# The first pass of a decoder trunk's first SwiGLU layer, written anew: modulation sums on TensorE, another order of each step

## The chip, the cores and the metric

The kernel runs on one core of a Trainium2 chip. The metric is the device time of one execution in microseconds (us), the median of several executions. The engines of the core are TensorE (PE in the profile; PEld is its weight loading), VectorE (DVE), ScalarE (ACT), GpSimd (POOL) and SyncE (SP), which issues most of the transfers.

## The reference

Two layers act on 512 tokens of width 1024 in fp32. Each has a SwiGLU half-step, a mixing step and another SwiGLU half-step, and each of these begins with an RMS norm and a modulation whose shift and scale come from a conditioning vector `c`. Only the head of the first half-step matters here:

```
h    = rms_norm(x, g)                        # x: (1, 512, 1024)
ada  = silu(c) @ ada_w + ada_b               # 9 x 1024 numbers a layer: shift, scale, gate of three steps
h    = h * (1.0 + scale) + shift             # per column of the 1024
out  = (silu(h @ w_gate) * (h @ w_up)) @ w_down     # w_gate, w_up: 1024 x 2816
```

`silu(c) @ ada_w` is a product of a vector with a matrix: each of its numbers is a sum over 1024 rows of `ada_w`, which come from memory 1 MB at a time.

## The kernel before

**Layout.** `x` is kept transposed, as eight tiles x0 to x7 of 128 columns (on the partitions) by 512 tokens. A product with a weight matrix is made in blocks: 128 rows of the weight by 128 output columns are the stationary operand, 512 tokens stream past it. fp32 accuracy comes from three products in a reduced format (fp32r): `mac` issues hi·hi (L302), hi·lo (L303: weight hi, data lo) and lo·hi (L304: weight lo, data hi) for each block. A weight's hi part is a cast on ACT (L284), its lo part a subtraction on DVE, or on POOL for an item with `pool_low` (both L286). An *item* is the weight for 128 output columns with all eight row blocks; `gu[0]`, `gu[1]`, ... are those of gate and up in turn (even ones gate, odd ones up).

**Order.** The whole program is one list of calls, `self.plan`; every engine takes its instructions in the order in which the list issues them, and semaphores join the engines. Raw weights arrive in four buffers of 1 MB (`RAW_BUFS`), loaded on SP's queue in the order of use; a buffer is loaded again once all uses of what it held have been issued. `hold` keeps a lo part back until `release`; `late` splits an item only where the list says `pre`.

**The first pass.** The modulation of this first half-step can't be had before `ada_w` lands, so the pass goes column block by column block. For block `d` (128 of the 1024 columns), `first_blocks` makes shift and scale from one raw buffer [128, 8, 2, 128] (row block k, shift or scale j):

- `scaled(d)`: three terms on ACT (L1516), raw times one number of `silu(c)` per partition;
- `products(d)`: the other five on DVE (L1524) into two of the three sums, and two additions that join the three (L1527, L1528; on DVE for d up to 1, on POOL after that);
- `sums(d)`: the sum over the partitions, two one-column products on PE with a vector of ones (L1535), and three small DVE operations that make `modB` (the shift, L1539) and `modA` ((1 + scale)·g, L1540, L1541).

Then `apply` modulates that column block: `t = x·modA·rb` on DVE (L575; `rb` is the reciprocal norm of each token), `hh = t + modB` rounded on ACT (L578), and `hl`, what the rounding left, on DVE (L580, kept back until `low`). Its 512-token products follow: 12 for the four *lead* items (`gu[0]` to `gu[3]`), and from column 1 on (`JOIN`) also 9 for the three *join* items (`gu[4]` to `gu[6]`), which have caught up on column 0 by then. Over all eight columns that is 168 products. The next item, `gu[7]`, follows with all its columns at hand. In every step the list issues `sums(k + 1)` and `apply(k + 1)` **ahead of** the products of column k, so that column k's 21 products run on PE while DVE and ACT make column k + 1. Everything behind the first pass is the same code before and after.

## Time and profile before

| | us |
|---|---|
| time, median of 3 runs (1841.98 to 1844.58) | 1843.25 |
| profiled execution, own time | 1845.38 |
| profiled execution, span of the trace | 1843.6 |
| TensorE busy in the span | 1794.6 |
| first pass: first 512-token product starts | 23.08 |
| `gu[7]`'s first product starts | 83.12 |

The span is the time from the first to the last instruction in the trace; the execution's own time has 1.8 us around it. Durations below are those of one instruction in the trace; since PE's instructions overlap their neighbours, what a product costs in a run is the distance from one start to the next. A window's "PEclk" is TensorE's granted clock as a share of full speed: 1.00 is 2.4 GHz, 0.50 is 1.2 GHz.

### The profile page before, as it was taken

The page shows a single profiled execution, that of the slowest core. Times are in us where ns is not written, and L with a number is a line of the kernel's source. Part 1 is how long each engine was busy: PE and PEld are TensorE (multiplying, and loading weights), DVE is VectorE, ACT ScalarE, POOL GpSimd, SP SyncE. Part 2 cuts the span into 40 slices and gives each one's busy share as a digit, 9 for nine tenths or more (in the row PEclk, how much of TensorE's full clock was granted, in tenths as well). Part 3 has the DMA queues.
Part 4 walks back from the last instruction along what each step waited for, and adds up shares of the span by engine and source line. Part 5 has one row for each costly group of instructions (what it writes and reads, how often), then busy time and mean ns, then how long its engine had stood idle before and what let it go on. Part 6 is the DMA issues. An engine that isn't in the chain of part 4 may idle for free.

```text
span 1843.6 us, 26711 instructions
## 1 busy us (share of the span) xinstructions
PE 1794.6 (97%) x10730; PEld 1563.4 (85%) x10730; DVE 1411.1 (77%) x2084; ACT 816.1 (44%) x1404; POOL 144.5 (8%) x123
## 2 busy tenths in 40 slices
PE   5999999999999999999999999999999999999998
PEld 3787889988778888989888889998866788898997
DVE  6689879775797869799677787886898586485874
ACT  4322325447754433436344234453545444253543
POOL 2100000005760000000000000000002000000000
PEclk7999999999999999999999999999999999999999
DMA  9585564447752346353423664543462132424321
GB/s 253 164 295 205 172 187 122 138 115 164 166 177 88 115 162 196 123 148 105 160 71 113 218 210 136 145 133 97 134 205 71 54 92 69 114 81 126 92 92 46
DMA packets 275940, 255.93 MB, mean 139 GB/s; under 512 B 5628, under 2 KB 254312, under 8 KB 275816
## 3 DMA queue, kind: packets, MB, share of 16 engines
q1 hardware_dynamic: 273380, 245.78, 43.5%
q0 software_dynamic: 2304, 8.39, 2.5%
q8 instruction: 84, 1.38, 0.3%
q14 instruction: 40, 0.33, 0.1%
q10 hardware_dynamic: 132, 0.05, 0.0%
HBM read 243.72 MB, written 2.10 MB: 133 GB/s over the span
## 4 chain that ended last, share of the span: by engine, by line
PE 81%; DVE 10%; ACT 3%; issue 2%; POOL 2%; DMA 1%; SPq 0%; ACTq 0%; POOLq 0%; DVEq 0%
PE bank L791 30%; PE bank L302 16%; PE bank L304 16%; PE bank L303 16%; DVE hl L580 1%; DVE wlo L286 1%; DVE adaacc L487 1%; DMA raw<-in_ada_w_dram 1%; ACT whi L284 1%; DVE t L575 1%; POOL y L1124 1%; DVE pm L1362 1%; DVE x L1010 1%; DVE p L1359 0%; DVE acc L1524 0%
## 5 line engine op out<-in xcount | busy, mean ns | idle before, releaser
L302 PE MATMUL bank<-th,whi 128*128 128x512 f32 (+1 forms) x896 | 336.6, 376 | 0.7 <-ACT th L1404 0.7
L304 PE MATMUL bank<-th,wlo 128*128 128x512 f32 (+1 forms) x896 | 333.9, 373 | 2.7 <-POOL wlo L286 2.7
L303 PE MATMUL bank<-tl,whi 128*128 128x512 f32 (+1 forms) x896 | 333.4, 372 | 1.1 <-DVE tl L687 0.9
L302 PE MATMUL bank<-hh,whi 128*128 128x512 f32 (+1 forms) x864 | 322.1, 373 | 5.5 <-ACT hh L578 3.2
L303 PE MATMUL bank<-hl,whi 128*128 128x512 f32 (+1 forms) x864 | 316.6, 366 | 8.1 <-DVE hl L580 8.1
L304 PE MATMUL bank<-hh,wlo 128*128 128x512 f32 (+1 forms) x864 | 315.8, 366 | 3.2 <-DVE wlo L286 2.6
L284 ACT CAST whi<-raw 128x1024 fp32r<-128x1024 f32 (+1 forms) x205 | 204.4, 1012 | 135.8 <-PE bank L303 83.3
L286 DVE TENSOR_TENSOR wlo<-raw,whi 128x1024 fp32r<-128x1024 f32 (+1 forms) x179 | 209.4, 1187 | 19.1 <-ACT whi L284 18.4
L304 PEld LDWEIGHTS bank<-th,wlo 128*128 128x128 f32 x896 | 169.4, 189 | 36.1 <-POOL wlo L286 4.3
L303 PEld LDWEIGHTS bank<-tl,whi 128*128 128x128 f32 x896 | 169.6, 189 | 32.3 <-DVE tl L687 1.3
L302 PEld LDWEIGHTS bank<-th,whi 128*128 128x128 f32 x896 | 169.6, 189 | 32.0 <-ACT th L1404 0.9
L303 PEld LDWEIGHTS bank<-hl,whi 128*128 128x128 f32 x864 | 163.4, 189 | 37.9 <-DVE hl L580 9.6
L302 PEld LDWEIGHTS bank<-hh,whi 128*128 128x128 f32 x864 | 163.6, 189 | 36.9 <-ACT hh L578 3.3
L304 PEld LDWEIGHTS bank<-hh,wlo 128*128 128x128 f32 x864 | 163.7, 189 | 33.2 <-DVE wlo L286 3.7
L1010 DVE SCALAR_TENSOR_TENSOR x<-bank,modG,x 128x512 f32<-128x512 f32 (+1 forms) x124 | 85.7, 698 | 133.2 <-PE bank L304 132.3
L791 PE MATMUL bank<-f,qhi 128*128 128x256 f32 x896 | 165.3, 282 | 0.0
L791 PE MATMUL bank<-f,whi 128*128 128x256 f32 x896 | 163.0, 280 | 0.2
L748 ACT CAST qhi<-raw 128x512 fp32r<-128x512 f32 x168 | 100.7, 621 | 111.9 <-issue 77.1
L487 DVE SCALAR_TENSOR_TENSOR adaacc<-raw,cond,adaacc 128x1024 f32<-128x1024 f32 x112 | 143.7, 1283 | 2.7
L791 PEld LDWEIGHTS bank<-f,whi 128*128 128x128 f32 x896 | 137.6, 188 | 1.9 <-ACT yy L851 0.9
L791 PEld LDWEIGHTS bank<-f,qhi 128*128 128x128 f32 x896 | 138.7, 190 | 0.0
L791 PE MATMUL bank<-f,qlo 128*128 128x256 f32 x448 | 126.5, 282 | 0.2 <-DVE qlo L751 0.2
(247 smaller groups left out, 3334.8 us busy)
## 6 DMA issues: line engine op xcount, KB each, us to landing
raw<-in_ada_w_dram SPq DMA_DIRECT2D x64, 1024.0 KB, 5.0
raw<-in_ffn_w_down_dram SPq DMA_DIRECT2D x32, 1024.0 KB, 5.5
raw<-in_ffn_w_gate_dram SPq DMA_DIRECT2D x58, 512.0 KB, 4.1
raw<-in_ffn_w_up_dram SPq DMA_DIRECT2D x58, 512.0 KB, 5.3
raw<-in_ffn_w_gate_dram SPq DMA_DIRECT2D x15, 1024.0 KB, 5.4
raw<-in_ffn_w_up_dram SPq DMA_DIRECT2D x15, 1024.0 KB, 5.4
raw<-in_ffn_w_down_dram SPq DMA_DIRECT2D x16, 768.0 KB, 4.4
raw<-in_conv_w_in_dram SPq DMA_DIRECT2D x20, 512.0 KB, 5.9
```

Source lines behind the costliest of these rows:

```text
L284: self.nc.scalar.copy(hi[:, 0:n, :], w)
L286: low = lambda eng=eng, lo=lo, hi=hi, w=w, n=n: eng.tensor_tensor(lo[:, 0:n, :], w, hi[:, 0:n, :].bitcast(F32), op=ALU.subtract)
L302: nc.tensor.matmul(ps, lhsT=it.hi[k], rhs=xh[:, sl], start=start, stop=False)
L303: nc.tensor.matmul(ps, lhsT=it.hi[k], rhs=xl[:, sl], start=False, stop=False)
L304: nc.tensor.matmul(ps, lhsT=it.lo[k], rhs=xh[:, sl], start=False, stop=stop)
L487: nc.vector.scalar_tensor_tensor(acc, r.tile[:, j, :], self.cond[:, k:k + 1], acc, op0=ALU.mult, op1=ALU.add)
L575: nc.vector.scalar_tensor_tensor(t, self.x[k][:, sl], self.modA[:, i, k:k + 1], rb, op0=ALU.mult, op1=ALU.mult)
L580: self.pend = lambda: nc.vector.scalar_tensor_tensor(self.hl[k][:, sl], t, b, self.hh[k][:, sl].bitcast(F32), op0=ALU.add, op1=ALU.subtract)
L748: self.nc.scalar.copy(hi, src)
L791: mm = lambda w, x, start=False: nc.tensor.matmul(ps, lhsT=w, rhs=x, start=start, stop=False, skip_group_check=True)
L1010: nc.vector.scalar_tensor_tensor(self.x[d][:, sl], ps[:, sl], self.modG[:, i, d:d + 1], self.x[d][:, sl], op0=ALU.mult, op1=ALU.add)
L1124: nc.gpsimd.tensor_tensor(y, y, m, op=ALU.add)
```

## The change

Only the first pass is changed.

- **Sums.** `by_pe(d)` says how many of the eight terms stay on ACT and DVE: 2, 2, 3, 5, 6, 6, 6, 6 for d = 0 to 7, the first on ACT, the others on DVE into the same sum. PE makes the rest: one-column fp32 products with the raw block as the stationary operand and a column of `silu(c)` as the moving one, and one with ones for the sum of ACT and DVE (L1559), for the scale (j = 1) first and then the shift. Per column that is 14, 14, 12, 8, 6, 6, 6, 6 one-column products, 72 in all, where there were 2 each, 16 in all. The additions on DVE and POOL are gone. `modA` is now one DVE operation (L1561; `one_b`, 1 + bias, is made once), `modB` one on ACT (L1563).
- **Order.** `sums(k + 1)` and `apply(k + 1)` stand **behind** the lead products of column k, and the join products between `apply(k + 1)` and the lead products of column k + 1. The join items start later and apart (`JOINS`: at k = 2, 4 and 7) and run one column behind. With column 1 only `gu[0]` and `gu[2]` go on; `gu[1]` and `gu[3]` take columns 0 and 1 together.
- **Buffers.** The three join items' raw weights go into buffers that are idle then (`fetch_home`), not into the ring of four.
- **Products that nothing reads.** `busy(n)` issues n products of the identity with itself (L1527): 8 while x arrives, 4 ahead of the norm's spread, 6 behind `sums(0)` and 6 behind `sums(1)`.

```diff
+    def fetch_home(self, items):
+
+        for it in items:
+            r, n = it.raw, len(it.raw.home)
+            r.tile = []
+            for e, tag in enumerate(r.home):
+                if tag == "s13":
+                    t = self.fp.tile([P, 2, S], F32, name=tag, tag=tag, bufs=1).rearrange("p a b -> p (a b)")
+                elif tag == "adaacc":
+                    t = self.fp.tile([P, D], F32, name=tag, tag=tag, bufs=1)
+                else:
+                    t = self.fp.tile([P, S], F32, name=tag, tag=tag, bufs=3)
+                t = t.rearrange("p (a b) -> p a b", b=P)
+                self.nc.sync.dma_start(t, r.src[:, e * ND // n:(e + 1) * ND // n, :])
+                r.tile += [t[:, a:a + 4, :] for a in range(0, ND // n, 4)]
...
+            w = src[i] if isinstance(src, list) else src[:, i * step:(i + 1) * step, :]
...
+        self.busy(BUSY[0])
...
+            nc.vector.tensor_scalar(self.one_b, self.adabT[:, 0, 8:16], 1.0, None, op0=ALU.add)
...
+    def busy(self, n):
+
+        ps = self.bank()
+        for _ in range(n):
+            self.nc.tensor.matmul(ps[:, 0:P], lhsT=self.ident, rhs=self.ident, start=True, stop=True)
+        self.free(ps)
...
         def scaled(d):
             def go():
-                st[d] = acc = [self.fp.tile([P, S], F32, name=f"acc{e}", tag=SPARE[d % 3 * 3 + e], bufs=1)
-                               [:, 0:256].rearrange("p (a b) -> p a b", a=2) for e in range(3)]
-                for k in range(3):
-                    nc.scalar.activation(acc[k], raws[d].tile[:, k], AF.Copy, scale=self.cond[:, k:k + 1])
+                st[d] = acc = self.fp.tile([P, S], F32, name="acc0", tag=SPARE[d % 3], bufs=1)[
+                    :, 0:256].rearrange("p (a b) -> p a b", a=2)
+                nc.scalar.activation(acc, raws[d].tile[:, 0], AF.Copy, scale=self.cond[:, 0:1])
             return go
 
         def products(d):
             def go():
                 acc = st[d]
-                for k in range(3, 8):
-                    a = acc[k % 2]
-                    nc.vector.scalar_tensor_tensor(a, raws[d].tile[:, k], self.cond[:, k:k + 1], a,
+                for k in range(1, by_pe(d)):
+                    nc.vector.scalar_tensor_tensor(acc, raws[d].tile[:, k], self.cond[:, k:k + 1], acc,
                                                    op0=ALU.mult, op1=ALU.add)
-                eng = nc.gpsimd if d > DMERGE else nc.vector
-                eng.tensor_tensor(acc[2], acc[2], acc[0], op=ALU.add)
-                eng.tensor_tensor(acc[2], acc[2], acc[1], op=ALU.add)
             return go
 
         def sums(d):
             def go():
                 ps = self.bank()
-                for j in range(2):
-                    nc.tensor.matmul(ps[:, j:j + 1], lhsT=st[d][2][:, j, :], rhs=self.ones[:, 0:1],
-                                     start=True, stop=True)
-                b = self.adabT[:, 0, d:d + 1], self.adabT[:, 0, 8 + d:9 + d]
-                m = self.modA[:, 0, d:d + 1]
-                nc.vector.tensor_tensor(self.modB[:, 0, d:d + 1], ps[:, 0:1], b[0], op=ALU.add)
-                nc.vector.scalar_tensor_tensor(m, ps[:, 1:2], 1.0, b[1], op0=ALU.add, op1=ALU.add)
-                nc.vector.tensor_tensor(m, m, self.g_of(0, 0)[:, d:d + 1], op=ALU.mult)
+                for j in (1, 0):
+                    terms = [(raws[d].tile[:, k, j, :], self.cond[:, k:k + 1]) for k in range(by_pe(d), 8)]
+                    terms.append((st[d][:, j, :], self.ones[:, 0:1]))
+                    for n, (w, c) in enumerate(terms):
+                        nc.tensor.matmul(ps[:, j:j + 1], lhsT=w, rhs=c, start=n == 0,
+                                         stop=n == len(terms) - 1)
+                nc.vector.scalar_tensor_tensor(self.modA[:, 0, d:d + 1], ps[:, 1:2], self.one_b[:, d:d + 1],
+                                               self.g_of(0, 0)[:, d:d + 1], op0=ALU.add, op1=ALU.mult)
+                nc.scalar.activation(self.modB[:, 0, d:d + 1], ps[:, 0:1], AF.Identity,
+                                     bias=self.adabT[:, 0, d:d + 1], scale=1.0)
...
-        for it, q in zip(join, (4, 6, 2)):
+        for it, home in zip(join, (("s13",), ("adaacc",), ("qlo", "qlo"))):
+            it.raw.home = home
+        for it, q in zip(join, (4, 2, 6)):
             it.store = [(self.th[q + e], self.tl[q + e]) for e in range(2)]
             it.late = True
         for it in [(lead + join)[e] for e in LOWS]:
@@ -1566,38 +1591,55 @@
         def ready(k):
             return lambda: self.apply(0, k, FULL, self.rb0)
         self.call(lambda: self.start_copy(range(7)))
-        self.call(scaled(0))
-        self.call(products(0), raws[0])
+        self.call(lambda: self.busy(BUSY[1]))
         self.call(self.start_spread)
+        self.call(scaled(0), raws[0])
+        self.call(products(0))
         self.call(self.early)
         self.call(lambda: self.start_copy((7,)))
         for e in HOLD:
             lead[e].hold = True
+        lead[1].late = lead[3].late = True
+        self.call(sums(0), raws[0])
+        self.call(lambda: self.busy(BUSY[2]))
+        self.call(lambda: self.fetch_home(join[:1]))
+        self.pre([lead[0]])
+        self.call(ready(0))
+        self.call(self.low)
         self.pre([lead[0], lead[2]])
-        self.call(sums(0))
-        self.call(ready(0))
         self.call(self.release)
-        self.call(self.low)
         self.call(scaled(1), raws[1])
-        self.call(products(1), raws[1])
+        self.call(products(1))
         self.outer([lead[0], lead[2]], 0, None, True, False)
-        self.pre(lead)
-        if EARLY:
-            self.call(self.release)
+        fetches = [lambda e=e: self.fetch_home(join[e:e + 1]) for e in (1, 2)]
         for k in range(ND):
+            if k > 1:
+                self.outer(lead, k, None, False, k == 7)
+            if k < 2:
+                self.call(fetches[k])
+            if k + 1 < ND:
+                self.call(sums(k + 1), raws[k + 1])
+                if k == 0:
+                    self.call(lambda: self.busy(BUSY[3]))
+                self.call(ready(k + 1))
+                self.call(self.low)
+            if k == 0:
+                self.outer([lead[0], lead[2]], 1, None, False, False)
+                self.pre(lead)
+                self.call(self.release)
+            for it, first in zip(join, JOINS):
+                if k == first - 1:
+                    self.pre([it])
             if k + 2 < ND:
                 self.call(scaled(k + 2), raws[k + 2])
-            if k + 1 < ND:
-                self.call(sums(k + 1))
-                self.call(ready(k + 1))
-            self.call(self.release)
-            if k + 2 < ND:
-                self.call(products(k + 2), raws[k + 2])
-            self.call(self.low)
-            self.outer(lead if k else [lead[1], lead[3]], k, None, k == 0, k == 7)
-            if k >= JOIN:
-                for q in range(0 if k == JOIN else k, k + 1):
-                    self.outer(join, q, None, q == 0, q == 7)
+                self.call(products(k + 2))
+            if k == 0:
+                for q in range(2):
+                    self.outer([lead[1], lead[3]], q, None, q == 0, False)
+            for it, first in zip(join, JOINS):
+                if k >= first:
+                    for q in range(0 if k == first else k - 1, k if k < 7 else 8):
+                        self.outer([it], q, None, q == 0, q == 7)
...
-JOIN = 1
+JOINS = (2, 4, 7)
+BUSY = (8, 4, 6, 6)
+def by_pe(d):
+    return (2, 2, 3, 5)[d] if d < 4 else 6
```

Three places show the new order. On TensorE, around the first column's sums (`bank_279`/`bank_272`: sums of column 0; `hh_101`, `hl_109`: column 0; `acc`: the sum that ACT and DVE made), before:

```order
L1498 MATMUL bank_256<-ident,rs_162 128x128 x4
L419 MATMUL bank_263<-ident,par 128x32
L420 MATMUL bank_263<-ident,adab 128x72
L1535 MATMUL bank_279<-ones,acc_242 128x1 x2
L302 MATMUL bank_312<-hh_101,whi 128x512
L303 MATMUL bank_312<-hl_109,whi 128x512
L304 MATMUL bank_312<-hh_101,wlo 128x512
L302 MATMUL bank_316<-hh_101,whi 128x512
L303 MATMUL bank_316<-hl_109,whi 128x512
L304 MATMUL bank_316<-hh_101,wlo 128x512
L1535 MATMUL bank_328<-ones,acc_292 128x1 x2
```

The same place now (column 1's sums write `bank_329`):

```order
L1517 MATMUL bank_255<-ident,rs_172 128x128 x4
L436 MATMUL bank_265<-ident,par 128x32
L437 MATMUL bank_265<-ident,adab 128x72
L1559 MATMUL bank_272<-cond,raw 128x1 x6
L1559 MATMUL bank_272<-ones,acc_262 128x1
L1559 MATMUL bank_272<-cond,raw 128x1 x6
L1559 MATMUL bank_272<-ones,acc_262 128x1
L1527 MATMUL bank_292<-ident 128x128 x6
L318 MATMUL bank_319<-hh_101,whi 128x512
L319 MATMUL bank_319<-hl_109,whi 128x512
L320 MATMUL bank_319<-hh_101,wlo 128x512
L318 MATMUL bank_323<-hh_101,whi 128x512
```

The two sums of a column have become fourteen products with raw weights and ones, and the unread products with `ident` stand behind them. In the middle of the pass, TensorE at the sums of column 6 before (`bank_580`); `hh_105` is column 4, `hh_106` column 5:

```order
L303 MATMUL bank_414<-hl_113,th_120 128x512
L304 MATMUL bank_414<-hh_105,tl_128 128x512
L1535 MATMUL bank_580<-ones,acc_530 128x1 x2
L302 MATMUL bank_312<-hh_106,whi 128x512
L303 MATMUL bank_312<-hl_114,whi 128x512
L304 MATMUL bank_312<-hh_106,wlo 128x512
L302 MATMUL bank_348<-hh_106,whi 128x512
L303 MATMUL bank_348<-hl_114,whi 128x512
L304 MATMUL bank_348<-hh_106,wlo 128x512
L302 MATMUL bank_316<-hh_106,whi 128x512
```

and now (`bank_578`; `bank_319`, and others of its kind, belong to the lead items, `bank_468` and `bank_553` to the join items):

```order
L320 MATMUL bank_385<-hh_106,wlo 128x512
L1559 MATMUL bank_578<-cond,raw 128x1 x2
L1559 MATMUL bank_578<-ones,acc_543 128x1
L1559 MATMUL bank_578<-cond,raw 128x1 x2
L1559 MATMUL bank_578<-ones,acc_543 128x1
L318 MATMUL bank_468<-hh_105,th_122 128x512
L319 MATMUL bank_468<-hl_113,th_122 128x512
L320 MATMUL bank_468<-hh_105,tl_130 128x512
L318 MATMUL bank_553<-hh_105,th_120 128x512
L319 MATMUL bank_553<-hl_113,th_120 128x512
L320 MATMUL bank_553<-hh_105,tl_128 128x512
L318 MATMUL bank_319<-hh_107,whi 128x512
```

Before, the products of column 5 followed the sums of column 6 at once; now only the joins' six stand between the sums of column 6 and lead products that need column 6. On VectorE in the same part of the program, before (`t_448` and `hl_112`: column 3):

```order
L1539 TENSOR_TENSOR modB<-bank_442,adabT 128x1
L1540 SCALAR_TENSOR_TENSOR modA<-bank_442,adabT 128x1
L1541 TENSOR_TENSOR modA<-modA,vec 128x1
L575 SCALAR_TENSOR_TENSOR t_448<-x_96,modA,sq 128x512
L1524 SCALAR_TENSOR_TENSOR acc_437<-raw,cond,acc_437 128x256
L1524 SCALAR_TENSOR_TENSOR acc_436<-raw,cond,acc_436 128x256
L1524 SCALAR_TENSOR_TENSOR acc_437<-raw,cond,acc_437 128x256
L1524 SCALAR_TENSOR_TENSOR acc_436<-raw,cond,acc_436 128x256
L1524 SCALAR_TENSOR_TENSOR acc_437<-raw,cond,acc_437 128x256
L580 SCALAR_TENSOR_TENSOR hl_112<-t_448,modB,hh_104 128x512
L1539 TENSOR_TENSOR modB<-bank_488,adabT 128x1
```

and now:

```order
L594 SCALAR_TENSOR_TENSOR t_457<-x_96,modA,sq 128x512
L599 SCALAR_TENSOR_TENSOR hl_112<-t_457,modB,hh_104 128x512
L1548 SCALAR_TENSOR_TENSOR acc_461<-raw,cond,acc_461 128x256 x5
L1561 SCALAR_TENSOR_TENSOR modA<-bank_487,one_b,vec 128x1
L594 SCALAR_TENSOR_TENSOR t_498<-x_97,modA,sq 128x512
L599 SCALAR_TENSOR_TENSOR hl_113<-t_498,modB,hh_105 128x512
```

The five additions for a later column stood between `t` and `hl` of a column; now `hl` follows `t`, and the additions follow `hl`.

## Rows read from the trace of the kernel before

**Rows 1.** The profile's page: busy time of TensorE, its granted clock in 40 slices of the span (tenths), and the chain that ended last by engine.

```profile
PE 1794.6 (97%) x10730; PEld 1563.4 (85%) x10730; DVE 1411.1 (77%) x2084; ACT 816.1 (44%) x1404; POOL 144.5 (8%) x123
...
PEclk7999999999999999999999999999999999999999
...
PE 81%; DVE 10%; ACT 3%; issue 2%; POOL 2%; DMA 1%; SPq 0%; ACTq 0%; POOLq 0%; DVEq 0%
```

**Rows 2.** Windows of the first pass by stage. Columns: window, its length, then busy time (and instructions) of PE, PEld, DVE, ACT, POOL, then granted clock, DMA share, GB/s.

```profile
14.90:18.00 3.10, 0.00 (x0) 0.00 (x0) 2.12 (x6) 2.33 (x6) 0.00 (x0) 0.93 1.16 316
18.00:23.00 5.00, 0.99 (x4) 0.93 (x4) 3.90 (x9) 2.62 (x4) 2.35 (x1) 0.50 1.14 323
23.00:26.50 3.50, 3.17 (x6) 1.78 (x6) 3.47 (x9) 3.17 (x6) 0.00 (x0) 0.50 1.18 292
26.50:34.70 8.20, 4.24 (x11) 2.51 (x10) 6.38 (x12) 3.42 (x8) 4.30 (x3) 0.50 1.00 250
34.70:41.40 6.70, 6.65 (x18) 5.39 (x19) 5.53 (x12) 3.84 (x7) 2.59 (x3) 0.50 0.42 116
41.40:44.80 3.40, 1.14 (x6) 0.61 (x4) 3.40 (x3) 0.02 (x1) 2.73 (x2) 0.99 1.00 264
44.80:48.30 3.50, 3.50 (x9) 2.73 (x10) 0.48 (x1) 1.30 (x3) 0.00 (x0) 0.51 1.16 308
48.30:82.00 33.70, 33.50 (x152) 26.30 (x150) 20.86 (x48) 9.49 (x18) 7.67 (x8) 1.00 0.58 168
```

**Rows 3.** TensorE's waits from 12 to 90 us: line, engine and tile waited for; total, times, longest.

```profile
PE bank L1535 <- DVE acc L1528: 4.4, 2, 4.1
PE bank L302 <- ACT hh L578: 3.2, 1, 3.2
PE bank L304 <- DVE wlo L286: 2.6, 2, 2.0
PE bank L304 <- DVE tl L286: 2.3, 1, 2.3
PE bank L1535 <- POOL acc L1528: 1.6, 1, 1.6
```

**Rows 4.** Timeline of the start: start, duration, engine, line, operation, count, and idle time before with what ended it.

```profile
14.93 1.31 ACT L1516 ACTIVATE acc<-raw,cond 128x256 f32<-128x256 f32 x3 [0.86 <-DMA raw<-in_ada_w_dram]
15.88 2.07 DVE L1524 SCALAR_TENSOR_TENSOR acc<-raw,cond,acc 128x256 f32<-128x256 f32 x5 [1.55 <-ACT acc L1516]
...
18.89 0.99 PE L1535 MATMUL bank<-ones,acc 128*128 128x1 f32 x4 [4.08 <-DVE acc L1528]
19.05 2.35 POOL L286 TENSOR_TENSOR wlo<-raw,whi 128x1024 fp32r<-128x1024 f32 x1 [5.34 <-ACT whi L284]
...
22.31 0.72 ACT L578 ACTIVATE hh<-t,modB 128x512 fp32r<-128x512 f32 x1 [2.38 <-DVE t L575]
...
23.08 0.80 PE L302 MATMUL bank<-hh,whi 128*128 128x512 f32 x1 [3.21 <-ACT hh L578]
23.32 0.75 DVE L580 SCALAR_TENSOR_TENSOR hl<-t,modB,hh 128x512 fp32r<-128x512 f32 x1
...
24.57 2.00 ACT L284 CAST whi<-raw 128x1024 fp32r<-128x1024 f32 x2 [0.33 <-DMA raw<-in_ffn_w_up_dram]
...
25.14 0.63 PE L302 MATMUL bank<-hh,whi 128*128 128x512 f32 x1
...
25.57 0.63 PE L303 MATMUL bank<-hl,whi 128*128 128x512 f32 x1
...
26.96 0.93 PEld L1535 LDWEIGHTS bank<-ones,acc 128*128 128x128 f32 x4 [1.06 <-issue]
...
27.77 0.33 PEld L302 LDWEIGHTS bank<-hh,whi 128*128 128x128 f32 x1
```

**Rows 5.** Timeline of one step at full clock, around the sums of a column in the middle of the pass.

```profile
54.93 0.52 PEld L1535 LDWEIGHTS bank<-ones,acc 128*128 128x128 f32 x4 [0.47 <-POOL acc L1528]
...
55.37 0.19 PEld L302 LDWEIGHTS bank<-hh,whi 128*128 128x128 f32 x1
...
55.57 0.16 DVE L1539 TENSOR_TENSOR modB<-bank,adabT 128x1 f32<-128x1 f32 x1 [1.30 <-PE bank L1535]
...
55.72 0.40 PE L303 MATMUL bank<-hl,whi 128*128 128x512 f32 x1
...
55.83 0.16 DVE L1541 TENSOR_TENSOR modA<-modA,vec 128x1 f32<-128x1 f32 x1
55.95 0.39 PE L304 MATMUL bank<-hh,wlo 128*128 128x512 f32 x1
...
56.03 0.75 DVE L575 SCALAR_TENSOR_TENSOR t<-x,modA,sq 128x512 f32<-128x512 f32 x1
...
56.81 0.73 ACT L578 ACTIVATE hh<-t,modB 128x512 fp32r<-128x512 f32 x1 [3.70 <-DVE t L575]
```

**Rows 6.** TensorE's timeline at another place of the kernel, where eight narrow fp32 weight loads and products run in a row.

```profile
488.06 0.95 PE L1183 MATMUL bank<-blk,sq 128*128 128x2 f32 x8
488.88 0.48 PE L302 MATMUL bank<-hh,whi 128*128 128x512 f32 x1
```

**Rows 7.** TensorE's timeline at the first and the third product of `gu[7]`.

```profile
83.12 0.50 PE L302 MATMUL bank<-hh,whi 128*128 128x512 f32 x1 [0.87 <-ACT whi L284]
...
84.38 0.50 PE L304 MATMUL bank<-hh,wlo 128*128 128x512 f32 x1 [0.53 <-DVE wlo L286]
```

More of the change, by code (lines that the diff above doesn't have):

```diff
@@ L39, in __init__ @@
         self.shape, self.src, self.uses = shape, src, uses
-        self.tile = None
+        self.tile = self.home = None
 class Item:
@@ L144, in touch @@
                 def touch(r):
-                    if id(r) not in known:
+                    if r.home is None and id(r) not in known:
                         known.add(id(r))
@@ L154, in used @@
                     touch(r)
-                else:
+                elif r.home is None:
                     uses[id(r)] -= 1
@@ L281, in split @@
         for i, (hi, lo) in enumerate(parts):
-            w = src[:, i * step:(i + 1) * step, :]
+            w = src[i] if isinstance(src, list) else src[:, i * step:(i + 1) * step, :]
             n = w.shape[1]
@@ L442, in setup @@
         self.early, self.fetch, self.rest = early, fetch, rest
+        self.one_b = cp.tile([P, ND], F32, name="one_b")
         self.modA = cp.tile([P, 6, ND], F32, name="modA")
@@ L1507, in first_blocks @@
         w = self.a["ada_w"][0].rearrange("(k p) (t e) -> p k t e", p=P, t=9)
-        raws = [Raw([P, 8, 2, P], w[:, :, 0:2, d * P:(d + 1) * P], 2 - (d == 0)) for d in range(ND)]
+        raws = [Raw([P, 8, 2, P], w[:, :, 0:2, d * P:(d + 1) * P], 2) for d in range(ND)]
         st = {}
@@ L1730 @@
 HOLD = (1, 2)
-DMERGE = 1
 EARLY = 0
```

## The prediction

> **What bounds the kernel now.** I read the page first: TensorE is busy for 97% of the span and makes 81% of the chain that ended last [rows 1]. So the reader looks for time in which PE does no 512-token product, or does it slowly. The granted clock is below full only in the first of the 40 slices [rows 1]; everything that is changed ends at `gu[7]`, about 84 us in, and behind that the code and the order are the same. I therefore compare one point, the start of `gu[7]`, before and after; what it moves by, the end moves by, since PE is the bound from there on.
>
> The windows [rows 2] split the first pass. At full clock a 512-token product takes 0.23 us from start to start (55.72 to 55.95, [rows 5]), at half clock 0.43 (25.14 to 25.57, [rows 4]). Before 48.3 us the clock is mostly at 0.50: PE runs 6 products and then parts of two windows with 11 and 18 instructions at half, and 9 more at 0.51 after a dip. Less the eight sums instructions that the middle two hold, some 36 products lose 0.20 each, about 7 us, and the first sums about 0.4 a pair: 8 us go to the clock. From 48.3 to 82 PE is busy 33.5 of 33.7 us at full clock: there is nothing to gain there.
>
> The waits [rows 3]: 4.1 us for the first column's `acc` on DVE, 3.2 for the first `hh`, 2.0 and 2.3 for lo parts on DVE, 1.6 for `acc` on POOL, and the rest short ones. The pass so consists of 168 products, 16 one-column products, the half clock and waits. `gu[7]`'s first product starts at 83.12 after a wait, and its third at 84.38 after another [rows 7]; as if all ran on from the third, it starts at 84.38 - 0.46 = 83.92.
>
> **The change, part by part.**
>
> *One-column products.* 72 instead of 16. A pair costs 0.44 (55.37 - 54.93, four weight loads, [rows 5]); in a run of eight loads 0.82 (488.06 to 488.88, [rows 6]), that is 0.205 for a product of two loads; at half clock 0.405 (26.96 to 27.77, [rows 4]). 72 x 0.205 = 14.8 us against 3.5: **11.3 us more of PE's time**, all on the path, as nothing else can stand in its place on PE. What it costs with a raw block as stationary operand no row shows. From above it is 0.22 (the pair alone, halved: 15.8 us in all); from below, if one of its two loads hid beside the other, 0.10 (7.4 us in all). I take 0.205, since the loads of [rows 6] have the same shape and type. The additions on DVE and POOL that go are off the path once the first `acc` is there (DVE's additions cost 0.41 each, [rows 4], and stand behind `hl` now).
>
> *The chain behind the sums.* Before, column k's 21 products cover it. After, `modA` waits for the last one-column product, S. From [rows 5]: the first small DVE operation starts 0.17 to 0.20 after the last sum, `t` 0.2 later (one operation instead of three), `hh` 0.78 after that (56.03 to 56.81) and takes 0.73, PE starts about 0.05 later: S + 1.93. `hl` takes 0.75 (23.32, [rows 4]) from S + 1.91, so the second product, which reads it, starts at S + 2.72. Twelve lead products then end at S + 5.27 when nothing covers them. Join products between them only fill the 1.9 us, they don't add.
>
> *The start.* The first fourteen one-column products begin when the raw block lands (14.93, [rows 4]), no longer at 18.89: S0 = 14.93 + 2.87 = 17.80. `hh` waits for a cast on ACT as well, so the first product starts near 20.3 instead of 23.08. POOL's lo part (2.35 us, [rows 4]) behind that cast holds the third; the six products of column 0 end at 23.1. Column 1: S1 = 23.1 + 2.87 = 26.0, second product 28.7, six end 29.9. `gu[1]` and `gu[3]` land at 24.57 [rows 4]; their casts (1.0 each) now stand behind column 1's `hh`, which ends at 27.5, so POOL's lo part of `gu[3]` ends about 32 (27.5 + 2.0 + 2.35); with the seven of their twelve products that are left then, 33.9.
>
> *The steps at full clock.* S2 = 33.9 + 12 x 0.205 = 36.4. Column 2 has nothing to cover it: S3 = 36.4 + 5.27 + 8 x 0.205 = 43.3. S4 = S3 + 5.27 + 6 x 0.205 = 49.8. S5 = S4 + 5.27 + 1.23 + 0.4 for an `acc` that five additions make late = 56.7. At k = 4 fifteen join products (3.5 us) hide the chain: S6 = 56.7 + 27 x 0.232 + 1.23 = 64.2. S7 = 64.2 + 6.5 = 70.7. The last lead products end at 75.9, 36 join products take 8.35, and `gu[7]` starts at **84.3**; its parts are ready by then, so the waits of [rows 7] are gone. Against 83.92 that is **+0.4**: 11.3 us of sums, 2.5 at most of unread products behind the two first sums (12, each no dearer than a 512-token one) that lie in the chain's wait, and about 13 us of chain waits, against 8 of clock and 16 of old waits.
>
> *The clock.* That is for a clock that holds. The rows: at the start it is high, then goes to 0.50 while PE does nothing until the first sums (window 14.9 to 18 at 0.93 with no PE work, 18 to 23 at 0.50 with 0.99 us busy). It doesn't rise in 26.5 to 34.7, with PE busy for 4.24 of 8.2 us, part of it one-column products. It is back at 0.99 in 41.4 to 44.8, behind a window in which PE was busy 6.65 of 6.7. And there, with PE busy for 1.14 of 3.4 us around a single wait of 2.3 [rows 3], it is lost again: 0.51 in the next [rows 2]. After the change the first 17 us have nothing to hurt more; but from 23.1 to 28.6 PE has one 512-token product at most, else fourteen one-column and six unread ones, and from 33.9 to 39 twelve one-column ones and one wide. Whether narrow products count as work no row shows alone. Bounds: they count in full, no loss (+0.4); they count for nothing, loss in both places and at the start. The nearest row is the dip at 44 us, so I take a loss in both later places: fourteen sums at 0.405 instead of 0.205, the products of column 1 and a part of the next twelve at 0.43 instead of 0.23, of which the wait for POOL absorbs some: sums 2 start near 36.7 (**+2.8**); around column 2 some eight products at half clock: **+1.6**. Sum: 0.4 + 2.8 + 1.6 = **+4.8**. If the first fall stays at 17.5 too, column 0's six products and the unread ones add 1.9.
>
> The Trainium skill, page "TensorE: Matmul & The Clock Gate", section "Why this matters for your kernels", advises to keep the engine busy and to leave no long idle gap between bursts of products, and names an idle gap as what takes the clock. With the unread products the gaps here are short, so by that page the clock would hold and the result be the +0.4. The trace differs from it in one place: one wait of 2.3 us between products sufficed [rows 2, 3].
>
> **Transfers.** About 10.5 MB stand behind the first block on SP's queue; at 0.25 to 0.32 MB per us [rows 2] the last block lands near 50 to 55 us, well ahead of column 7's sums at 64. Hidden.
>
> **The rivals.**
> A. *The clock holds* (the unread products do what narrow work can): +0.4 us. For it: a window with PE busy got the clock back. Against: the dip at 44.
> C. *The clock falls at the first sums too*, as before: +6.7. For it: the first window of [rows 2].
> F. *The chain starts at the scale's column, not at the last product.* The scale is summed first; if `t` starts when it is there, the shift's seven to three one-column products run beside DVE's `modA` and `t`: (7 + 7 + 6 + 4 + 3 + 3 + 3) x 0.205 = 6.8 us off the +0.4 at full clock, about **-6.2**; faster from some 4.1 us saved. Against it: `modA` is written after the whole group in the list, and in [rows 5] the DVE operation that reads the second sum stands with the first behind the pair. A shorter price for the one-column products would act the same way: it takes 0.06 us a product.
> D. *No change*: each gain is taken back. It is A's number.
>
> **How the numbers follow.** The sum is against the profiled execution's own 1845.4 us (span 1843.6): 1850.2. That is 2.1 above the median of the runs, 1843.25; the shift of +4.8 carried to the median gives **1848.0**. 0.2% is 3.7 us, about what a measurement of this kernel tells from no change. Chances: the forecast B 0.48, A 0.22, C 0.12, F 0.14, rest 0.04. B is uncertain by 2 either way (a quarter of it falls within 3.7); A by 2.5. Faster: F, 0.02 of A and 0.02 of the rest, 0.18. Same: 0.20 of A, 0.12 of B, 0.02 of the rest: 0.34. Slower: 0.36 of B and C: 0.48. The range goes from 1841.0 (A's lower edge, which leaves out F) to 1851.5 (C with 1.5 more); for B alone it is 1846 to 1850.
>
> **What would show it.** In the profile after: first 512-token product at 20 to 21 us; granted clock near 0.5 from 24 to 34 and again around 39 to 44; PE idle before `hh` in each step by 1 to 2.5 us except where the fifteen join products stand; steps of 6.5 to 7.5 us against 5.6 before (33.7 us for six columns, [rows 2]); no wait at `gu[7]`; its start near 88.7 us. It is wrong if one-column products take far from 0.2, if the clock is at 1.0 throughout (then the start is 84 to 85), or if `t` starts before the shift's products have ended.

## Result and the profile after

The changed kernel is slower: 1861.89 us (median of 4 runs, 1860.59 to 1866.14) against 1842.83, a ratio of 1.0106 (95% interval 1.0091 to 1.0121). The forecast was 1848.0, with a range up to 1851.5. The profiled execution has a span of 1858.8 us, 15.2 more than that of before, while the medians differ by 19.1: the profiled execution of before took 2.55 us more than this median of before, and the one here 1.30 less than its own. The page, its lines that answer to [rows 1]:

```profile
span 1858.8 us, 26972 instructions
...
PE 1818.2 (98%) x10890; PEld 1588.2 (85%) x10890; DVE 1401.9 (75%) x2053; ACT 811.3 (44%) x1396; POOL 132.1 (7%) x111
...
PEclk8999999999999999999999999999999999999999
...
PE 81%; DVE 10%; ACT 4%; issue 2%; POOL 2%; DMA 1%; SPq 0%; POOLq 0%; ACTq 0%; DVEq 0%
```

TensorE is as full as before and its clock even better; the loss must lie in more work, or in dearer work. Windows of the first pass, cut where the granted clock changes (columns as in [rows 2]), and TensorE's waits (as [rows 3]):

```profile
14.10:18.00 3.90, 3.90 (x35) 3.88 (x35) 1.28 (x6) 1.56 (x5) 0.00 (x0) 1.00 1.11 346
18.00:23.60 5.60, 3.02 (x15) 2.14 (x15) 4.44 (x4) 2.99 (x5) 2.36 (x1) 0.90 1.11 362
23.60:32.40 8.80, 8.80 (x43) 8.71 (x41) 1.53 (x3) 1.58 (x3) 0.00 (x0) 0.50 1.03 302
32.40:38.00 5.60, 4.69 (x20) 3.58 (x20) 4.28 (x4) 1.70 (x3) 2.46 (x1) 0.97 0.48 140
38.00:43.00 5.00, 3.09 (x26) 2.83 (x24) 1.32 (x3) 1.36 (x3) 0.00 (x0) 1.00 1.10 324
43.00:46.40 3.40, 3.15 (x8) 2.37 (x8) 3.29 (x7) 1.06 (x3) 0.00 (x0) 0.50 0.89 265
46.40:91.40 45.00, 40.97 (x201) 32.57 (x201) 25.95 (x47) 14.89 (x27) 2.60 (x2) 1.00 0.40 125
```

```profile
PE bank L318 <- ACT hh L597: 5.0, 6, 1.9
PE bank L319 <- DVE hl L599: 3.3, 6, 1.9
PE bank L320 <- POOL wlo L302: 0.9, 1, 0.9
PE bank L1559 <- DVE acc L1548: 0.5, 1, 0.5
```

The clock is at half from 22.5 to 32.8 and from 43.0 to 46.4, 14 us in place of 27 [rows 2]. The waits have changed as forecast: the long one for the first `acc` is gone, one for `hh` and one for `hl` stand in nearly every step. The places that answer to [rows 4, 5 and 7], first the start (four rows of the timeline), then one step, then `gu[7]`:

```profile
19.10 2.36 POOL L302 TENSOR_TENSOR wlo<-raw,whi 128x1024 fp32r<-128x1024 f32 x1 [5.82 <-ACT whi L300]
...
19.68 2.33 DVE L599 SCALAR_TENSOR_TENSOR hl<-t,modB,hh 128x512 fp32r<-128x512 f32 x1 [1.10 <-ACT hh L597]
...
19.70 0.49 PE L318 MATMUL bank<-hh,whi 128*128 128x512 f32 x1 [0.71 <-ACT hh L597]
...
22.06 0.50 PE L319 MATMUL bank<-hl,whi 128*128 128x512 f32 x1 [1.87 <-DVE hl L599]
```

```profile
54.68 0.51 PE L1559 MATMUL bank<-cond,raw 128*128 128x1 f32 x4
...
55.72 0.36 PE L1559 MATMUL bank<-ones,acc 128*128 128x1 f32 x2
...
57.99 0.51 PE L318 MATMUL bank<-hh,whi 128*128 128x512 f32 x1 [1.11 <-ACT hh L597]
58.78 0.51 PE L319 MATMUL bank<-hl,whi 128*128 128x512 f32 x1 [0.28 <-DVE hl L599]
```

```profile
91.41 0.39 PE L318 MATMUL bank<-hh,whi 128*128 128x512 f32 x1
```

The sums start at 14.1, the first 512-token product at 19.70 (23.08 before), but the second waits until 22.06 for `hl`, which takes 2.33 us on DVE while POOL makes a lo part. In the step, the sums end at 55.94, three join products follow, then waits of 1.11 and 0.28. `gu[7]` starts without a wait at 91.41: **8.3 us later than in [rows 7]**, 7.4 to 7.5 when the two waits there are counted in.

So half of the 15.2 us lies behind the first pass, where no order and no instruction was changed. The place of [rows 6] shows it on the way (the same sums, 406 us behind `gu[7]`):

```profile
497.50 0.95 PE L1202 MATMUL bank<-blk,sq 128*128 128x2 f32 x8
```

488.06 has become 497.50, a lag of 9.4 us; from `gu[7]` to the end the lag grows evenly (this growth is called the drift below), but for two places where the clock of before is at half. Behind `gu[7]` a 512-column product takes 234.2 ns from start to start. The first and the 61st of a run without a gap in this kernel, 14.05 us for 60:

```profile
102.42 0.40 PE L320 MATMUL bank<-hh,wlo 128*128 128x512 f32 x1
...
116.47 0.40 PE L320 MATMUL bank<-hh,wlo 128*128 128x512 f32 x1
```

### The profile page after: what moved, and what is told of

Same layout as the page of the kernel before. It is cut to its first block, busy times and chain, and to the rows that moved or that the text cites. A ratio compares the mean times of both kernels' runs of the same rounds, so it can differ in the third digit from the quotient of the medians.

```text
span 1858.8 us, 26972 instructions
## 1 busy us (share of the span) xinstructions
PE 1818.2 (98%) x10890; PEld 1588.2 (85%) x10890; DVE 1401.9 (75%) x2053; ACT 811.3 (44%) x1396; POOL 132.1 (7%) x111
## 4 chain that ended last, share of the span: by engine, by line
PE 81%; DVE 10%; ACT 4%; issue 2%; POOL 2%; DMA 1%; SPq 0%; POOLq 0%; ACTq 0%; DVEq 0%
PE bank L810 30%; PE bank L319 16%; PE bank L318 16%; PE bank L320 16%; DVE hl L599 2%; DVE adaacc L506 1%; DVE wlo L302 1%; PE bank L1559 1%; ACT whi L300 1%; DVE t L594 1%; DVE pm L1381 1%; POOL y L1143 1%; DVE p L1378 1%; POOL wlo L302 1%; ACT hh L597 1%
## 5 line engine op out<-in xcount | busy, mean ns | idle before, releaser
L302 DVE TENSOR_TENSOR wlo<-raw,whi 128x1024 fp32r<-128x1024 f32 (+1 forms) x179 | 208.9, 1183 | 20.1 <-ACT whi L300 19.1
L319 PEld LDWEIGHTS bank<-hl,whi 128*128 128x128 f32 x864 | 163.4, 189 | 42.2 <-DVE hl L599 13.7
```

Of the source, the lines that this page charges most:

```text
L302: low = lambda eng=eng, lo=lo, hi=hi, w=w, n=n: eng.tensor_tensor(lo[:, 0:n, :], w, hi[:, 0:n, :].bitcast(F32), op=ALU.subtract)
L319: nc.tensor.matmul(ps, lhsT=it.hi[k], rhs=xl[:, sl], start=False, stop=False)
```

## Experiments

The kernel before was measured again beside each group of experiments: 1842.8 to 1843.5 us. Ratios are to that.

**Addresses.** A program places its tiles one behind the other. The new tile `one_b` (32 bytes in each partition) stands ahead of the raw and weight tiles and moves them up by 32 bytes: `whi` from 122336 to 122368, while `hh`, `hl`, `th` and `tl` stay (`hh` at 19616). Theory 1: this makes every product dearer. Rival 2: the new first pass does.

e1 puts an unused tile of the same size into the kernel before:

```diff
+        self.pad = cp.tile([P, ND], F32, name="pad")
         self.modA = cp.tile([P, 6, ND], F32, name="modA")
```

> The kernel before with one unused tile of 32 bytes per partition allocated where the changed kernel has one_b (ahead of modA), so that the raw, hi and lo weight tiles lie 32 bytes higher, at the very addresses of the changed kernel; no instruction differs. Behind the first pass the changed kernel's trace falls back by another 7.8 us, evenly over the rest of the program (a product's start-to-start 233.3 ns before, 234.2 after). Theory 1 (addresses): this kernel shows that drift alone: 7 to 10 us above the kernel before, start-to-start 234.2 ns, first product and gu[7] as before (23.1, 83.1). Rival 2 (the drift comes with the new first pass, its instruction count or the moments at which the clock changes): within 2 us of the kernel before, 233.3 ns.

Measured: 1854.99 us, ratio 1.0063 (1.0051 to 1.0075): +12.1. Not one instruction is added, `gu[7]` stands where it stood, and the sums of [rows 6] are 2.0 us late (490.10); at the end the lag is 8.4 (span 1852.0). The other 3.7 lie in which executions were profiled: that of before 2.5 above its median, that of e1 1.2 below. The first row is `gu[7]`, the second from another window:

```profile
83.18 0.50 PE L302 MATMUL bank<-hh,whi 128*128 128x512 f32 x1 [0.87 <-ACT whi L284]
...
490.10 0.95 PE L1184 MATMUL bank<-blk,sq 128*128 128x2 f32 x8
```

e2 takes the shift out of the changed kernel:

```diff
-        self.one_b = cp.tile([P, ND], F32, name="one_b")
+        self.one_b = self.vec[:, 96:96 + ND]
```

> The changed kernel with one_b in eight unread columns of the tile vec, so that all weight tiles lie where they lay before; order and products as in the changed kernel. Theory 1: 1852 to 1855 us, start-to-start back at 233.3 ns, gu[7] at about 91 us as in the changed kernel, and no drift behind it. Rival 2: 1861 us, 234.2 ns.

Measured: 1854.27 us, 1.0057 (1.0044 to 1.007), 7.6 below the changed kernel and 11.4 above before. `gu[7]` starts at 92.38, no earlier, and the drift is gone: `gu[7]` is 8.5 behind before (with the waits there counted in), and the end 8.3, by the spans. Sixty products take 14.00 us, 233.3 ns each:

```profile
102.42 0.39 PE L319 MATMUL bank<-hl,whi 128*128 128x512 f32 x1
...
116.42 0.39 PE L319 MATMUL bank<-hl,whi 128*128 128x512 f32 x1
```

Theory 1 stands. The new first pass as a whole (sums, order, buffers and unread products) costs 8.3 us by itself in the traces, 11.4 in the medians. e3, e7, e8 and e16 ask what of the address counts; they move tiles by other amounts (one_b as [P, 16]; the unused tile as [P, 48]; one of [P, ND] ahead of x; cond and mx moved ahead of x).

> The changed kernel with one_b twice as large, so that the weight tiles lie 64 bytes higher than before instead of 32. Theory 1 with a period of 64 bytes: 1852 to 1855 us, 233.3 ns. Theory 1 with a longer period or none: the drift stays in another size. Rival 2: 1861 us, 234.2 ns.

> The kernel before with an unused tile of 192 bytes ahead of modA: raw and weight tiles move by 192 bytes, and then lie at the same address modulo 512 as the tiles hh, hl, th and tl. Products with weights in th ran in the changed kernel at 227 ns from start to start, those with weights in whi at 233 (no shift), 234 (32 bytes) and 232.5 (64 bytes). If the relative address of weight and data modulo 512 sets the rate: 227 ns all through, 30 to 45 us faster than before. If 32 bytes modulo 64 is all that counts: as before within 2 us. Otherwise some other rate, total between 1842 and 1862.

> The kernel before with an unused tile of 32 bytes ahead of x, so that data (x, hh, hl, th, tl) and weights all move by 32 bytes and keep their distance. If the distance of weight and data sets the rate: as before within 2 us (233.3 ns). If the weight's own address does: +10 to +13 us as in e1 (234.2 ns). If the data's address does: another rate.

> The kernel before with the two 32-byte tiles cond and mx allocated ahead of x instead of behind the data tiles: data tiles 64 bytes higher, weights where they were, so weight less data is 256 modulo 512 (0 modulo 256), where it was 320 before and is 0 in e7. If the distance counts modulo 256: the 512-column products run at 228 ns and the time is 6 to 12 us below the kernel before, as in e7. If modulo 512: another rate, and no such gain.

| run | whi less hh, modulo 256 | 512-column product, ns | 256-column, ns | total, us (ratio to before) |
|---|---|---|---|---|
| before, e2 | 64 | 233.3 | 117.0 | 1843, 1854.27 |
| e8, all moved by 32 | 64 | 233.3 | 117.0 | 1843.41 (0.9999, 0.999 to 1.0008) |
| changed, e1 | 96 | 234.2 | 118.0 | 1861.89, 1854.99 |
| e3 | 128 | 232.5 | 118.6 | 1861.59 (1.0099, 1.0086 to 1.0112) |
| e7 | 0 | 227.8 | 118.4 | 1834.28 (0.9955, 0.9941 to 0.9968) |
| e16 | 0 (256 modulo 512) | 227.7 | 118.4 | 1835.06 (0.9954, 0.994 to 0.9967) |

The nanoseconds are mean distances from one start to the next in stretches behind 100 us; a single run without a gap can lie up to 0.8 lower (e7's sixty below: 227.0). e8 says that for the 512-column products the distance of the two operands counts and not their place; e16, that a distance of 256 modulo 512 does as well as one of 0, since e7 and e16 agree. My three expectations for e7 all missed in size: the 512-column products became 5.5 ns cheaper, as the first said, but the 256-column ones 1.4 dearer, and 9 us were left. The 256-column figure is a mean over unlike kinds: in these traces (mean steps of 100 to 130 ns) those of `hh`, `hl`, `th` or `tl` with `whi` or `wlo` took 114.1 to 115.1 ns at a distance of 64, 117.4 to 118.5 at 96, 118.5 to 119.6 at 128 and 119.3 to 119.9 at 0, while those of `f` moved by 1.4 at most. For the former 64 was the cheapest of the four. The table's rates, times the 4296 products with 512 columns and 6048 with 256 that the trace holds, give an estimate of +9.9 us for e1, +6.2 for e3 against e2 and -15 for e7; measured were +12.1, +7.3 and -9.0, so the signs come out, the size of e7 doesn't. Sixty products of e7, 13.62 us:

```profile
117.52 0.39 PE L303 MATMUL bank<-hl,whi 128*128 128x512 f32 x1
...
131.14 0.39 PE L303 MATMUL bank<-hl,whi 128*128 128x512 f32 x1
```

e12 also put the tiles of the phase pool (f, qhi) at the same place modulo 512 (the tile tab moved to the pool ahead, 160 bytes of pad).

> The kernel before with 192 bytes (an unused tile of 160 and the one-number tile tab, moved from another pool) ahead of modA: raw and weight tiles at 160 modulo 512 as in e7, and the tiles of the phase pool (f, qhi and others) at 160 modulo 512 too, where they lay at 192 in e7 and at 0 before. 256-column products took 117.0 ns from start to start before, 118.4 in e7; those of the commonest short kind 113. If the relative address of the two operands sets the rate there as well: 113 to 115 ns and 10 to 20 us below e7 (1834.3). If not: 1834 within 2 us.

It missed: 1840.5 us (0.9983, 0.9974 to 0.9992), above e7, with 256-column products at 119.8 ns. For the 256-column products, equal places are not the cheapest; why, stays open. e13 gives the changed kernel e7's distance (one_b as [P, 48]).

> The changed kernel with one_b 192 bytes large instead of 32, so that raw and weight tiles lie at 160 modulo 512, like the data tiles, as in e7; nothing else differs from the changed kernel. If the distance of weight and data is all that the drift is: e2's time less what e7 gained, 1854.3 - 9.0 = 1845 (1843 to 1848), a 512-column product at 228 ns, and gu[7] at 91 to 92.5 us as in e2. Rival (the changed kernel drifts for another reason as well): above 1850.

1842.76 us (0.9996, 0.9987 to 1.0005), 0.2 below its range, the 512-column product at 227.8, `gu[7]` at 91.98: 160 bytes of unused space take 19.1 us off the changed kernel. The sum of the parts closes only roughly: e1's 12.1 and e2's 11.4 make 23.5, the change cost 19.1; at the layout of e7 and e13 the new first pass costs 8.5 (1842.76 against 1834.28). In the traces the drift is 7.8 to 8.4 and the first pass 7.4 to 8.5. But the trace of before is a late one: of the six traces with its first pass, at several layouts, `gu[7]` stands at 80.6 to 83.2, and against e8's 80.94, at the same distance of the operands, that of the changed kernel is 10.5 us later.

**The clock and the first pass.** e4 leaves out the 24 unread products (`BUSY = (0, 0, 0, 0)`).

> The changed kernel without its 24 unread products (BUSY all zero), nothing else changed. If the unread products hold TensorE's clock: the granted clock falls at 17 to 18 us instead of 22.5, some products of column 0 and the sums of column 1 run at half, gu[7] starts 1 to 3 us later, total +1 to +3 against the changed kernel. If they only lie in the way: the six behind column 1's sums ran at half clock until 32.4 and covered the chain; gu[7] up to 1 us earlier, total 0 to -1.

1862.73 us (1.0105, 1.0092 to 1.0118): no difference to the changed kernel in the time. In the trace the clock fell at 18.3 and stayed low for 20.5 us (10.2 in the changed kernel), and `gu[7]` came at 93.96. That the unread products hold the clock isn't shown by this: in e2, e3, e13 and e15, which have them and the same order, the clock fell at 16.2 to 17.2 and was at half for 20.5 to 23.9 us ahead of `gu[7]` (13.7 in the changed kernel, 27.3 in e4), with `gu[7]` at 91.88 to 92.60. Their worth is not clear of these differences.

e5 brings back one thing of the old order (at the old addresses): sums and modulation of column k + 1 ahead of the lead products of column k.

```diff
 for k in range(ND):
-    if k > 1:
-        self.outer(lead, k, None, False, k == 7)
...
     self.call(sums(k + 1), raws[k + 1])
     self.call(ready(k + 1))
     self.call(self.low)
...
+    if k > 1:
+        self.outer(lead, k, None, False, k == 7)
```

> The changed kernel with its tiles at the old addresses (one_b in vec, as in e2) and one thing of the old order: the sums and the modulation of column k + 1 stand ahead of the lead products of column k (for column 2 ahead of the twelve products of gu[1] and gu[3]), so that these cover the chain of modA, t, hh and hl. If the uncovered chain is what the new order costs (in the trace of e2 gu[7] starts 8.4 us later than before, with waits of 0.4 to 1.9 us for hh and 0.3 for hl in five steps): the waits for hh and hl behind column 1 vanish, gu[7] starts 6 to 9 us earlier than in e2, that is at 82 to 85 us; total 1842 to 1846 us. Rival (the one-column products and the clock at the start cost it, the chain waits are filled with something else): waits for acc on DVE take their place, gu[7] at 88 or later, total 1850 or more.

The waits for `hh` and `hl` went as the first theory says; the time, `gu[7]` and the new waits for `acc` are the rival's: 1852.74 us (1.0054, 1.0042 to 1.0067), `gu[7]` at 93.64. Waits and windows of e5:

```profile
PE bank L1559 <- DVE acc L1548: 3.8, 3, 2.4
PE bank L319 <- DVE hl L599: 1.3, 1, 1.3
```

```profile
16.60:37.10 20.50, 19.16 (x78) 17.77 (x79) 8.57 (x11) 6.43 (x10) 3.00 (x2) 0.50 1.07 291
37.10:40.50 3.40, 3.40 (x29) 3.27 (x28) 0.44 (x2) 0.23 (x1) 2.04 (x1) 1.00 0.17 47
40.50:43.90 3.40, 3.40 (x10) 2.60 (x9) 2.55 (x5) 2.20 (x5) 0.00 (x0) 0.50 0.90 245
43.90:47.30 3.40, 2.55 (x21) 2.35 (x20) 1.92 (x5) 0.00 (x0) 0.00 (x0) 1.00 1.19 290
47.30:50.70 3.40, 3.40 (x10) 2.64 (x9) 2.46 (x5) 1.38 (x3) 0.00 (x0) 0.51 1.17 320
50.70:61.00 10.30, 7.86 (x45) 6.73 (x44) 6.72 (x13) 2.43 (x5) 0.00 (x0) 1.00 0.47 127
61.00:67.80 6.80, 6.80 (x20) 5.55 (x20) 4.06 (x8) 1.38 (x3) 0.00 (x0) 0.50 0.46 155
67.80:93.60 25.80, 25.25 (x123) 21.09 (x122) 12.37 (x20) 9.70 (x16) 2.61 (x2) 1.00 0.34 119
```

The waits for `hh` are gone, one for `hl` and three for `acc` are left, 5.1 us in all. But TensorE is at half clock for 34 us in four stretches, after stretches in which it ran the sums or waited. What the order gave, the clock seems to have taken; e10 below tests it. e6 takes 22 of the one-column products away (`by_pe` 8 from column 3 on):

> As e2 (old addresses, new order), but columns 3 to 7 leave all eight terms to ACT and DVE (by_pe 2, 2, 3, then 8), so that PE makes 44 one-column products instead of 72 less 22 (50). If one-column products cost PE 0.2 us each on the path: 22 x 0.205 = 4.5 us less, less up to 1.5 for sums of DVE that come late: gu[7] 3 to 4.5 us earlier than in e2, total 1850 to 1852. If DVE's seven additions (0.41 each) come too late: waits for acc at each sum, no gain or a loss.

1851.67 us (1.0043, 1.0029 to 1.0057), 2.6 below e2 with overlapping ranges of runs, and in its trace `gu[7]` no earlier (93.13): half clock from 16.4 to 36.9, 43.7 to 50.5 and 60.7 to 64.2, waits for `acc` 1.8 us. So a gain from fewer products isn't shown. e9 leaves all as in e2, but lets each product of the sums stream its column 128 times:

```diff
-  terms = [(raws[d].tile[:, k, j, :], self.cond[:, k:k + 1]) for k in range(by_pe(d), 8)]
-  terms.append((st[d][:, j, :], self.ones[:, 0:1]))
+  terms = [(raws[d].tile[:, k, j, :], self.cond[:, k:k + 1].to_broadcast([P, P])) for k in range(by_pe(d), 8)]
+  terms.append((st[d][:, j, :], self.ones))
```

> As e2 (old addresses, new order), but each product of the sums streams its column 128 times (the vector's column broadcast to 128) instead of once; the same weight loads, the same sums. If TensorE's clock falls in the first pass because the 72 products stream only one column each: the clock stays high from the first sums on, at most one stretch of 3.4 us at half around column 2; per product up to 0.04 us more at full clock (an unread product of 128 columns took 0.26 us in the changed kernel, a one-column one 0.22), but no half rate: gu[7] at 86 to 89 us against 92.4 in e2, total 1846 to 1851. Rival (the waits between products bring the clock down): the clock falls as in e2, gu[7] at 93 to 96, total 1855 to 1858.

1850.18 us (1.0036, 1.0024 to 1.0049), 4.1 below e2. At full clock a product costs no more than with one column: column 2's twelve products, 24 weight loads, start between 37.74 and 40.30 (38.02 and 40.51 in the changed kernel). In e2 the clock was at half from 16.4 to 23.3, from 26.7 to 36.9 and from 43.7 to 47.1; its windows up to the second of these, then those of e9:

```profile
16.40:23.30 6.90, 6.55 (x30) 6.04 (x29) 2.37 (x3) 3.16 (x5) 1.98 (x1) 0.51 1.15 316
23.30:26.70 3.40, 2.42 (x15) 1.91 (x15) 2.46 (x3) 0.00 (x0) 0.38 (x1) 1.00 1.15 280
26.70:36.90 10.20, 10.20 (x42) 9.50 (x42) 4.78 (x5) 3.28 (x5) 2.20 (x1) 0.50 1.07 292
```

```profile
14.00:21.50 7.50, 5.40 (x42) 4.78 (x42) 3.47 (x7) 4.58 (x8) 2.18 (x1) 1.00 1.15 320
21.50:28.30 6.80, 6.01 (x23) 5.53 (x24) 2.27 (x3) 0.00 (x0) 0.18 (x1) 0.50 1.17 313
28.30:38.00 9.70, 7.80 (x45) 6.20 (x45) 5.80 (x6) 3.28 (x5) 2.46 (x1) 1.00 0.94 256
38.00:44.00 6.00, 3.80 (x28) 3.21 (x27) 2.50 (x5) 2.43 (x5) 0.00 (x0) 1.00 1.16 323
44.00:90.00 46.00, 41.67 (x205) 33.07 (x204) 27.85 (x50) 14.84 (x27) 2.61 (x2) 1.00 0.44 132
```

e9 has one stretch at half, 6.8 us, behind the wait for `hl`; most of column 1's sums lie in it (24.6 to 29.5), and there is none around column 2. With one-column products five traces of this order (the changed kernel, e2, e3, e13, e15) have 13.7 to 23.9 us at half ahead of `gu[7]`. `gu[7]` at 90.28 is short of what I expected, since the waits for `hh` and `hl` grew to 9.7 us. e10 has e5's order and e9's products.

> As e5 (old addresses, sums ahead of the lead products) with the sums' products 128 columns wide as in e9. In e5 the waits for hh and hl were gone but the clock was at half for 34 us of the first pass. If the clock is what took e5's gain: gu[7] at 80 to 84 us against 93.6, total 1840 to 1845. Rival (waits for acc, 3.8 us in e5, keep taking the clock): gu[7] at 88 to 92, total 1848 to 1853.

1847.48 us (1.0022, 1.0013 to 1.0032), 5.3 below e5, between the two ranges that were expected; `gu[7]` at 85.30, 8.3 earlier than in e5 (the profiled execution lies 2.6 below its median), with the clock at half for 3.4 us only, where e5 had 34.1 (3.4 and 6.8 in e11 and e14, which have the same products):

```profile
14.00:23.00 9.00, 6.05 (x46) 5.40 (x45) 5.08 (x8) 4.47 (x8) 2.37 (x1) 1.00 1.18 304
23.00:26.50 3.50, 3.50 (x16) 3.10 (x15) 0.65 (x2) 0.00 (x0) 0.00 (x0) 0.51 1.11 342
26.50:85.30 58.80, 51.99 (x280) 43.74 (x280) 34.32 (x61) 20.60 (x37) 5.27 (x3) 1.00 0.68 191
```

What is left to before, 4.0 us in the medians, are waits for `acc` (5.9 us, four), `hl` (2.2) and `hh` (1.4) and the price of the 72 products; no run parts them. e14 and e11 are e10 with the layouts of e7 and e12.

> e10 (sums ahead of the lead products, 128 columns wide) with the weight tiles 192 bytes higher, as in e7. If the causes add up: 1847.5 - 9.0 = 1838.5 (1836 to 1841), faster than both kernels, but not than e7 (1834.3), since gu[7] still starts at about 85 us.

> e10 with the layout of e12: hi, lo and raw weight tiles and the tiles of the phase pool at the same address modulo 512 as the data tiles. If address and clock are the two causes and add up: the time of e10 less what e12 gains against the kernel before, within 2 us; that is 1822 to 1836 and faster than both kernels.

e14: 1836.4 us (0.9962, 0.9948 to 0.9975), near the lower end of its range; faster than both kernels, but not than e7, which is the kernel before with 192 unused bytes. e11: 1844.12 (1.0001, 0.9992 to 1.001), outside its range, but e10 less what e12 gained is 1844.5: the causes add up; the range rested on a gain that e12 did not have.

e15 gives the lo part of `gu[0]` to DVE (`LOWS = (3, 6)`).

> e2 with the lo part of gu[0] on DVE instead of POOL. In the changed kernel hl of column 0 took 2.33 us on DVE while POOL made that lo part, 0.75 alone. If POOL's work beside it is the cause: hl takes 0.75 to 1.2 us, the second product starts 1.1 to 1.6 us earlier; the third then waits for DVE's lo part (1.2 us) and starts 0 to 0.7 earlier; in the total at most 1 us, within the noise. Rival (hl waits for something else): hl stays above 2 us.

`hl` takes 0.75 us, so POOL's subtraction beside it made the 2.33:

```profile
23.33 0.75 DVE L599 SCALAR_TENSOR_TENSOR hl<-t,modB,hh 128x512 fp32r<-128x512 f32 x1 [0.85 <-ACT hh L597]
```

But the lo part now stands ahead of `t` on DVE, the first product starts at 23.34, and nothing is gained: 1854.25 us (1.0061, 1.0048 to 1.0075), e2's time. The trace of before has the same thing: `modA`, 0.16 us in [rows 5], took 1.25 in the first column and ended at 21.42, as POOL's lo part of [rows 4] did (19.05 + 2.35):

```profile
20.17 1.25 DVE L1541 TENSOR_TENSOR modA<-modA,vec 128x1 f32<-128x1 f32 x1
```

## Why the prediction was wrong

**The step that failed** stands in its first part: "everything that is changed ends at `gu[7]`", and "what it moves by, the end moves by". It compared instructions and their order, not where their operands lie. The 32 bytes of `one_b` were in the diff. They cost 7.8 us in the trace (from 7.4 at `gu[7]` to 15.2 at the end), 7.6 in the time (changed kernel less e2). No rival named it, so the range could not hold it. It is not the whole miss: e2, without the shift, has 1854.27, also above 1851.5, so the first pass was mis-sized as well, and either error alone put the time outside the range.

**The first pass** went as described, with terms that were too small. Forecast for `gu[7]` was 88.7, measured 91.41; so of the 15.2 us in the traces 4.8 were forecast, 2.7 are the terms below and the rest is the drift. The other 3.9 up to the medians' 19.1 come from the forecast's step from single executions to the median: the one of before was 2.55 above its median, the one of the changed kernel 1.30 below.

- One-column products: 0.23 us each at full clock (28 rows of weight loads, 14 products, 14.10 to 17.37) against 0.205; at half 0.42: column 1's fourteen took 5.8 us (23.98 to 29.81), 5.7 forecast. Price and place were nearly right.
- The start: first product 19.70 (20.3 forecast), but the second at 22.06 instead of 0.8 us behind the first: `hl` beside POOL, 2.33 instead of 0.75. The prediction had priced it by a row without POOL at work, and did not use the `modA` of 1.25 us that stood beside POOL in the same trace. Sums 2 started at 38.02 instead of 36.7: 1.3 of the 2.7 us.
- The chain: `hh`'s product at S + 2.05 (1.93 forecast), the second at S + 2.84 (2.72), and steps of 6.78 and 7.5 us (6.5 and 6.9 to 7.5): the other 1.4 us.
- The clock: half near 24 to 34 and 39 to 44 forecast, 22.5 to 32.8 and 43.0 to 46.4 measured. Case B was the right case for this trace. In e2, e3, e13 and e15, with the same order, the clock fell ahead of column 0's products, at 16.2 to 17.2, which is rival C's condition; their `gu[7]` came 0.5 to 1.2 us later than here, where the prediction gave C 1.9 more. Rival A fell: from 18.0 to 23.6 TensorE was busy for 3.0 of 5.6 us, its longest wait 1.9, and the clock was lost; in e5 it was lost at 40.5 behind 3.4 us in which TensorE was busy throughout, with sums for the most part (window 37.1 to 40.5, PE 3.40 at 1.00, then 0.50). The Trainium skill, page "TensorE: Matmul & The Clock Gate", section "Why this matters for your kernels", advises to keep the engine busy and to leave no long idle gap between bursts; here that was not enough, since the longest wait ahead of the fall at 22.5 was 1.9 us.
- Rival F fell: `modA` starts when the last product of both columns has ended (17.58 after 17.54). Its own terms, 6.8 off +0.4, give -6.4, not -6.2.
- Transfers: hidden, as said; TensorE never waits for one after 14 us.

Signs that were named and came: no wait at `gu[7]`, the fifteen join products at column 4 without a wait, idle time ahead of `hh` in the other steps (0.4 to 1.9 us, where 1 to 2.5 were forecast).

## What to carry to other kernels

Look at what a diff does to the addresses of tiles, too: a small new tile ahead of the weights shifted all of them, and products with 512 columns took 0.9 ns more, those with 256 columns 1.0; put such a tile last, or try a few paddings: here 192 unused bytes took 9.0 us off the kernel before, while the new first pass cost time at each layout. Work that was moved onto TensorE as one-column products cost its weight loads here and then, by the clock, the speed of its neighbours; streamed 128 columns wide, the same products took no longer each, and the time was 4.1 and 5.3 us lower (e9, e10). A trace is one execution: compare its own time with the median before a shift of a few us is read from it. When a wait is taken out of a stretch and the time stays, read the granted clock of that stretch before looking for a new wait.
